# A ninth pair of the down product by seven products, with other low parts made by adding DMA

## The chip, the cores and the metric

The kernel runs on one core of a Trainium2 chip. The metric is the device time in microseconds (us). Before the change it is 286.42 us, the median of 3 runs (286.15 to 286.48). Beside it stands one profiled execution of 286.22 us, whose span from the first to the last instruction is 284.4 us; all rows of the trace come from that execution.

## The reference

One decoder layer in float32, for 256 tokens of width 1024: RMS norm, an input projection, eight heads of causal attention beside a convolution module, an output projection, and then the part that is changed, a SwiGLU feed-forward of width 2816:

```python
h = rms_norm(x, norm2_g[l])
x = x + (jax.nn.silu(h @ w_gate[l]) * (h @ w_up[l])) @ w_down[l]
```

## The kernel before, in words

**Split operands.** TensorE gets each float32 operand as two parts: a high part, which ScalarE makes by rounding (`activation(..., Copy)` into a float32r tile), and a low part, the original minus the high part. A product is then three matmuls: high by high, high by low, low by high. Each weight needs one rounding on ScalarE (L265 in `feed`, L200 in `split`) and one low part. The low part is made in one of two ways (`low_part`): VectorE subtracts (L219), or, for the pieces in the list `BY_DMA`, ScalarE writes the negated high part (L216) and a DMA issued by POOL adds the original to it (L217). The original comes from DRAM (`home`).

**Pieces and places.** The weights come from DRAM in blocks of 128 x 2048 through four buffers (`raw`). A piece is 128 x 1024. Pieces 0 to 71 belong to the projections and to gate and up; those from 72 (`DOWN`) on belong to the down product. Eight places (`WGT`) hold the split pieces; a new piece takes the place of the lowest numbered one, and ScalarE's rounding into it waits until TensorE has read that one for the last time. `feed(upto)` issues the roundings up to one piece past `upto` and the subtractions up to `upto`. `turns` is the order in which the pieces get their places: the number, except that a piece listed in `BEHIND` goes right behind the piece named there, to give its adding DMA time. Every engine executes in program order.

**Gate and up.** 22 blocks f of 128 feed-forward columns, 16 pairs of matmuls each. `glu_task` runs beside them: VectorE adds the halves of the gate (`tg`) and multiplies by the norm's factor, ScalarE makes silu of `tg` in a tile `sf`, VectorE adds the halves of the up product and multiplies by `sf`.

**The down product.** 11 pairs of feed-forward blocks. Seen as a product of 2 x 2 blocks (two halves of the tokens, two blocks of the pair, two halves of the 1024 columns), a pair marked P in `PAIRS` ("plain") is eight block products, 24 matmuls of 512 columns, and has two pieces. A pair marked F ("fast") is seven block products (`seventh`), 21 matmuls, with sums of blocks as operands. On the weights' side these sums are made by VectorE from the block of the pair in three instructions (`add_up`, L234 to L236, one of 1024 and two of 512 columns) into one of two buffers. A fast pair has three pieces, the raw second half of its block (a = 0) and the two halves of the sums (a = 1, 2), and the block's first quarter is split by itself (`single`, L200 and L201, into `b11` or `other`). On the activations' side, VectorE makes five sums (L869 to L871) and ScalarE and VectorE split seven operand forms (L875, L878); a plain pair has two splits instead (L860, L862). In the down product the pairs are run in order, 0 to 10. A fast pair takes its products in three groups; for all but the last fast pair the first group has the two products with piece a = 0 and then the first quarter's. The last fast pair, number 9, begins with the first quarter's product (M1), and then takes one with piece a = 1. Pair 10 is plain and is run last, one output block after the other, and VectorE adds each finished block to the residual stream (L981) while POOL adds others (L986). Ahead of these stand two sums of finished products on VectorE (L995, L997).

With `PAIRS = "FFFPFFFPFFP"` the pieces are 72 to 74 for pair 0, 75 to 77, 78 to 80, 81 and 82 for pair 3, 83 to 85, 86 to 88, 89 to 91, 92 and 93 for pair 7, 94 to 96, 97 to 99, 100 and 101 for pair 10. In the down product the issue order around pair 7 is: sums of pair 6, low parts 90, 91, 93, sums of pair 8, low part 94, quarter of pair 8, low parts 95 and 96, sums of pair 9, low part 97, quarter of pair 9, low parts 98 to 101.

Of the kernel before, what the change touches and what calls it, by code (L numbers as in the profile page):

```python
# [8 lines left out]
F32 = mybir.dt.float32  # L9
# [3 lines left out]
AF = mybir.ActivationFunctionType  # L13
ALU = mybir.AluOpType
AX = mybir.AxisListType

P = 128
D = 1024
T = 256
# [38 lines left out]
V_PIECE = 21  # L58
SS_WAIT = 2
OUT_LATE = 6  # L60
PAIRS = "FFFPFFFPFFP"
FAST = [p for p in range(NF // 2) if PAIRS[p] == "F"]
PLAIN = [p for p in range(NF // 2) if PAIRS[p] == "P"]
DOWN = 72
BEHIND = {75: 70, 78: 72, 81: 75, 82: 78, 83: 78, 86: 80, 89: 83, 92: 86}
BY_DMA = [*range(45, DOWN, 3), *BEHIND]
FAR = 46
SUMS = {66: 0, 69: 1}
FORMS_LATE = 11
# [72 lines left out]
def _build(nc, tc, t, ctx):  # L142
# [45 lines left out]
    def load_block(i, between=None):  # L188
        if i >= NB:
            return  # L190
        r = raw.tile([P, BW], F32, name=f"raw{i}", tag="raw")
        n = BW // (2 if between else 1)
        for j in range(BW // n):
            if j:
                between()
            nc.sync.dma_start(r[:, j * n:(j + 1) * n], t["w"][i - 2][:, j * n:(j + 1) * n])
        blocks[i] = r
# [5 lines left out]
    def new_piece():  # L203
        j = turns[len(pieces)]
        z = places.index(min(places))
        places[z] = j
        pieces[j] = [wgt.tile([P, PIECE], F32R, name=f"w{s}{j}", tag=f"w{s}{z}") for s in "hl"]
        i, a = divmod(j * PIECE, BW)
        if j >= DOWN:
            return pieces[j], down_piece(*down[j - DOWN]), j  # L210
        return pieces[j], blocks[i][:, a:a + PIECE] if i > 1 else None, j

    def low_part(dst, src, by_dma=False):

        if by_dma:
            nc.scalar.activation(dst[1], dst[0].bitcast(F32), AF.Copy, scale=-1.0)  # L216
            nc.gpsimd.dma_start(dst[1], src.bitcast(F32R), accum_op=ALU.add)  # L217
        else:
            nc.vector.tensor_tensor(dst[1], src, dst[0].bitcast(F32), op=ALU.subtract)  # L219
# [5 lines left out]
    index = {d: DOWN + a for a, d in enumerate(down)}  # L225
    turns = sorted(range(DOWN + len(down)), key=lambda j: BEHIND[j] + 0.5 if j in BEHIND else j)
    wsums, b11 = {}, {}
# [19 lines left out]
    def home(j):  # L247

        i, a = divmod(j * PIECE, BW)
        if j >= DOWN:  # L250
            p, a = down[j - DOWN]
            i, a = DOWN // 2 + p, (a if p in PLAIN else 1) * PIECE
        return t["w"][i - 2][:, a:a + PIECE]

    def single(q):

        i = DOWN // 2 + FAST[q]
        split(b11[q % 3], blocks[i][:, 0:W], nc.vector)
        load_block(i + RAW)

    def feed(upto, more=1):
        last = DOWN + len(down) - 1
        while len(pieces) <= min(upto + more, last):
            dst, src, j = new_piece()
            nc.scalar.activation(dst[0], src, AF.Copy)  # L265
            if j in BY_DMA:
                low_part(dst, home(j), True)
            waiting.append((dst, src, j))
            waiting.sort(key=lambda w: w[2])
        while waiting and waiting[0][2] <= upto:  # L270
            dst, src, j = waiting.pop(0)
            if j not in BY_DMA:
                low_part(dst, src)
            if j < DOWN and j % 2:
                load_block(j // 2 + RAW)
            elif j >= DOWN and down[j - DOWN][0] in FAST[2:] and down[j - DOWN][1] == 0:
                single(FAST.index(down[j - DOWN][0]))
            elif j >= DOWN and down[j - DOWN][0] in PLAIN and down[j - DOWN][1]:
                load_block(DOWN // 2 + down[j - DOWN][0] + RAW)
# [19 lines left out]
    def halves(out, bank, side):  # L299

        nc.scalar.activation(side, bank[:, T:], AF.Copy)
        nc.vector.tensor_tensor(out, bank[:, 0:T], side, op=ALU.add)
# [80 lines left out]
    for kt in range(KT):  # L383
        if kt % 2 == 0:
            dst, _, _ = new_piece()
# [260 lines left out]
    def ln_task():  # L646
# [5 lines left out]
        for i in (1, 0):  # L652
            b = t_bank(f"cv{i}", "s")
            for j in range(2):
                o = j * T + i * P
                mm3(b, [m[:, o:o + P] for m in inv], G["ys"][j], j == 0, i == 1 and j == 1)
            if i == 0:
                mm3(b, [m[:TAIL + 1, 2 * T:] for m in inv], G["ys"][2], False, True)
                cv[i] = b
            else:  # L660
                cv[i] = work("cvb", "tmp", 6)
                nc.vector.tensor_tensor(cv[i], b, G["glub"][:, 2, :], op=ALU.add)
            nc.vector.bn_stats(st[:, i, :], cv[i])
            nc.vector.bn_aggr(mv[:, i, :], st[:, i, :])
            if i:
                feed(V_PIECE + 1)
# [31 lines left out]
    for chunk in range(5):  # L698
        banks = [mm_bank(f"p{chunk}{i}") for i in range(NT)]
        for kt in range(KT):  # L700
            step()
            ahead = unit // 2 + 1 if unit < L1 else (unit + 3) // 2 if unit < L2 else unit // 2 + 3
            feed(ahead if unit < V_UNIT else min(ahead, V_PIECE))
            if unit == L1 - 1:
                feed(ahead + 1, 0)
            w = wtile(unit * W, W)
            unit += 1
            sls = [slice(i * P, (i + 1) * P) for i in range(NT)]
            order = [(i, a) for a in (0, 2, 1) for i in range(NT)]
            for i, a in order:  # L710
                nc.tensor.matmul(banks[i], (xh, xh, xl)[a][:, kt, sls[i]], w[a % 2], start=kt == 0 and a == 0,  # L711
                                 stop=kt == KT - 1 and a == 1)
        if after[chunk]:
            spawn(after[chunk](banks))
# [74 lines left out]
    for d in range(8):  # L789
# [3 lines left out]
        if d == 0:  # L793
            early_ctx.close()
            late = ffn["late"] = pool("late")
# [22 lines left out]
    late = ffn["late"]  # L818
# [19 lines left out]
    def glu_task(f, pg, pu):  # L838
        tg = late.tile([P, T], F32, name=f"tg{f}", tag="tg", bufs=2)
        halves(tg, pg, side(f"gs{f}"))  # L840
        nc.vector.tensor_tensor(tg, tg, r_bc, op=ALU.mult)
        s = late.tile([P, T], F32, name=f"sf{f}", tag="sf", bufs=2)
        yield 1
        nc.scalar.activation(s, tg, AF.Silu)
        yield max(1, ffn["up"][f] - now[0])
        pair, second = divmod(f, 2)
        if pair in PLAIN:
            ac = late.tile([P, T], F32, name=f"ac{f}", tag="ac")
        else:
            q = FAST.index(pair)  # L850
            if q not in pair_sums:
                pair_sums[q] = late.tile([P, 9 * P], F32, name=f"ps{q}", tag="ps")
            ps = pair_sums[q]
            ac = ps[:, 0:T] if second else ps[:, T:2 * T]
        halves(ac, pu, side(f"us{f}"))
        nc.vector.tensor_tensor(ac, ac, s, op=ALU.mult)
        if pair in PLAIN:
            a = 2 * PLAIN.index(pair) + second
            yield 1
            nc.scalar.activation(acts[:, 0, a, :], ac, AF.Copy)  # L860
            yield 1
            nc.vector.tensor_tensor(acts[:, 1, a, :], ac, acts[:, 0, a, :].bitcast(F32), op=ALU.subtract)  # L862
        elif second:
            if q == len(FAST) - 1:
                yield FORMS_LATE


            p3 = ps.rearrange("p (b q) -> p b q", q=P)
            nc.vector.tensor_tensor(p3[:, 4:6], p3[:, 2:4], p3[:, 0:2], op=ALU.subtract)  # L869
            nc.vector.tensor_tensor(p3[:, 6:8], p3[:, 5:6].to_broadcast([P, 2, P]), p3[:, 2:5:2], op=ALU.subtract)  # L870
            nc.vector.tensor_tensor(p3[:, 8], p3[:, 2], p3[:, 3], op=ALU.subtract)  # L871
            yield 1
            parts = ((forms[q][:, :, 0:3], p3[:, 0:3]), (forms[q][:, :, 3:7], p3[:, 5:9]))
            for to, of in parts:
                nc.scalar.activation(to[:, 0], of, AF.Copy)  # L875
            yield 1
            for to, of in parts:
                nc.vector.tensor_tensor(to[:, 1], of, to[:, 0].bitcast(F32), op=ALU.subtract)  # L878
# [4 lines left out]
    for f in range(NF):  # L883
# [5 lines left out]
        a = 0  # L889
# [20 lines left out]
        if f == 0:  # L910
            spawn(glu_task(0, pg, pu), GLU0_WAIT)
            ffn["up"][0] = now[0] + GLU0_WAIT
# [78 lines left out]
    m1, u1, u2, s = (rest[:, a, :] for a in range(4))  # L991
# [74 lines left out]
```

## Time and profile before

| | us | |
|---|---|---|
| median of the runs | 286.42 | 3 runs |
| profiled execution | 286.22 | one run |
| its span | 284.4 | |
| TensorE (PE) busy | 280.3 | 99% of the span |
| VectorE (DVE) busy | 236.0 | 83% |
| ScalarE (ACT) busy | 202.4 | 71% |
| POOL busy | 43.4 | 15% |
| DMA by the adding queue (POOL's) | | 18.0% of 16 engines' span |

A row in order of time has the start in us, the time taken, the engine, the line, the operation, what it writes and reads, and a count; in brackets stands the idle time ahead of it and what ended it. The low part of a weight is `wl`, the high part `wh`, the sums of a fast pair's weights `t`, the first quarter's parts `b11h`, `b11l` or, in the last pairs, `other`. The two parts of an operand of the activations are in `forms`, `other` or `act`.

### The profile page before, as it was taken

The page shows a single profiled execution, that of the slowest core. Times are in us where ns is not written, and L with a number is a line of the kernel's source. Part 1 is how long each engine was busy: PE and PEld are TensorE (multiplying, and loading weights), DVE is VectorE, ACT ScalarE, POOL GpSimd, SP SyncE. Part 2 cuts the span into 40 slices and gives each one's busy share as a digit, 9 for nine tenths or more (in the row PEclk, how much of TensorE's full clock was granted, in tenths as well). Part 3 has the DMA queues.
Part 4 walks back from the last instruction along what each step waited for, and adds up shares of the span by engine and source line. Part 5 has one row for each costly group of instructions (what it writes and reads, how often), then busy time and mean ns, then how long its engine had stood idle before and what let it go on. Part 6 is the DMA issues. An engine that isn't in the chain of part 4 may idle for free.

```text
span 284.4 us, 4150 instructions
## 1 busy us (share of the span) xinstructions
PE 280.3 (99%) x1466; PEld 235.0 (83%) x1466; DVE 236.0 (83%) x420; ACT 202.4 (71%) x331; POOL 43.4 (15%) x71
## 2 busy tenths in 40 slices
PE   8999999999999999999999999999999999999995
PEld 6887877778788888888888888888888888888884
DVE  4879996896894969999967687697489889999994
ACT  5857688986728677467878777776777799856640
POOL 0004555423000000000111111001111121200042
PEclk9999999999999999999999999999999999999999
DMA  7999958846204870746699998998996679994003
GB/s 265 381 421 367 410 178 291 316 156 213 84 0 149 309 277 7 296 151 235 214 305 293 304 288 229 279 285 218 332 214 158 179 241 281 267 303 186 0 0 148
DMA packets 12918, 65.62 MB, mean 231 GB/s; under 512 B 1697, under 2 KB 2305, under 8 KB 7266
## 3 DMA queue, kind: packets, MB, share of 16 engines
q1 hardware_dynamic: 10018, 55.14, 52.7%
q0 software_dynamic: 2736, 10.22, 18.0%
q8 instruction: 11, 0.18, 0.3%
q14 instruction: 9, 0.07, 0.1%
q10 hardware_dynamic: 144, 0.00, 0.0%
HBM read 64.31 MB, written 1.05 MB: 230 GB/s over the span
## 4 chain that ended last, share of the span: by engine, by line
PE 99%; DVE 0%; issue 0%
PE p L711 20%; PE sum L935 19%; PE fg L294 14%; PE fu L294 14%; PE po L757 8%; PE fg L296 7%; PE fu L296 7%; PE warm L356 1%; PE S L545 1%; PE pT L575 1%; PE O L731 1%; PE xT L770 1%; PE cv L305 0%; PE cv L307 0%; PE hf L305 0%; PE cv L306 0%
## 5 line engine op out<-in xcount | busy, mean ns | idle before, releaser
L265 ACT ACTIVATE wh<-raw 128x1024 fp32r<-128x1024 f32 x82 | 84.8, 1053 | 16.4 <-PE fu L294 7.8
L219 DVE TENSOR_TENSOR wl<-raw,wh 128x1024 fp32r<-128x1024 f32 x65 | 78.3, 1219 | 3.4 <-ACT wh L265 3.4
L294 PE MATMUL fu<-g,wh 128*128 128x512 f32 x176 | 62.5, 395 | 0.0
L294 PE MATMUL fg<-g,wh 128*128 128x512 f32 x176 | 62.4, 394 | 0.0
L296 PE MATMUL fg<-g,wl 128*128 128x256 f32 x176 | 48.8, 277 | 0.0
L296 PE MATMUL fu<-g,wl 128*128 128x256 f32 x176 | 48.8, 277 | 0.0
L217 POOL DMA_DIRECT2D wl<-w x17 | 14.7, 865 | 166.0 <-PE fu L296 70.8
L294 PEld LDWEIGHTS fg<-g,wh 128*128 128x128 f32 x176 | 33.0, 187 | 7.7
L294 PEld LDWEIGHTS fu<-g,wh 128*128 128x128 f32 x176 | 33.0, 188 | 7.6
L296 PEld LDWEIGHTS fg<-g,wl 128*128 128x128 f32 x176 | 33.1, 188 | 0.0
L296 PEld LDWEIGHTS fu<-g,wl 128*128 128x128 f32 x176 | 33.1, 188 | 0.0
L711 PE MATMUL p<-wh,xh 128*128 128x512 f32 x80 | 25.9, 405 | 0.0
L935 PE MATMUL sum<-wh,forms 128*128 128x512 f32 x84 | 25.8, 389 | 0.0
L711 PE MATMUL p<-wl,xh 128*128 128x512 f32 x80 | 24.9, 392 | 0.0
L711 PE MATMUL p<-wh,xl 128*128 128x512 f32 x80 | 24.8, 391 | 0.0
L265 ACT ACTIVATE wh<-t 128x1024 fp32r<-128x1024 f32 x16 | 16.9, 1057 | 9.4 <-PE sum L935 5.3
L219 DVE TENSOR_TENSOR wl<-t,wh 128x1024 fp32r<-128x1024 f32 x16 | 19.4, 1221 | 0.2
L216 ACT ACTIVATE wl<-wh 128x1024 fp32r<-128x1024 f32 x17 | 18.0, 1061 | 0.5
L935 PEld LDWEIGHTS sum<-wh,forms 128*128 128x128 f32 x84 | 15.7, 188 | 3.2
L711 PEld LDWEIGHTS p<-wh,xh 128*128 128x128 f32 x80 | 14.4, 190 | 4.2 <-issue 1.3
L711 PEld LDWEIGHTS p<-wl,xh 128*128 128x128 f32 x80 | 14.8, 188 | 3.6 <-DVE wl L219 0.5
L711 PEld LDWEIGHTS p<-wh,xl 128*128 128x128 f32 x80 | 15.0, 188 | 3.3
(203 smaller groups left out, 478.7 us busy)
## 6 DMA issues: line engine op xcount, KB each, us to landing
raw<-w SPq DMA_DIRECT2D x44, 1024.0 KB, 6.8
wl<-w POOLq DMA_DIRECT2D x17, 512.0 KB, 9.0
first<-first SPq DMA_DIRECT2D x8, 384.0 KB, 5.7
raw<-w SPq DMA_DIRECT2D x2, 512.0 KB, 7.1
xtok<-xtok SPq DMA_DIRECT2D x2, 512.0 KB, 9.7
x<-xtok SPq DMA_DIRECT2D x2, 512.0 KB, 6.6
c_rows<-rows SPq DMA_DIRECT2D x1, 768.0 KB, 11.0
out<-x SPq DMA_DIRECT2D x3, 256.0 KB, 2.0
```

Source lines behind the costliest of these rows:

```text
L216: nc.scalar.activation(dst[1], dst[0].bitcast(F32), AF.Copy, scale=-1.0)
L217: nc.gpsimd.dma_start(dst[1], src.bitcast(F32R), accum_op=ALU.add)
L219: nc.vector.tensor_tensor(dst[1], src, dst[0].bitcast(F32), op=ALU.subtract)
L265: nc.scalar.activation(dst[0], src, AF.Copy)
L294: nc.tensor.matmul(out.rearrange("p (a q) -> p a q", a=2), w[0], both, start=z in first and z not in seen, stop=False)
L296: nc.tensor.matmul(out[:, 0:T], w[1], both[:, 0, :], start=False, stop=z in last and left[z] == 0)
L356: nc.tensor.matmul(warm[:, 0:T], ones[:, 0:P], ones, start=True, stop=True)
L545: nc.tensor.matmul(banks[a][:, out], G["qT"][rows, j, q], G["kT"][rows, j, k], start=True, stop=True)
L575: nc.tensor.transpose(b[:, a * P:(a + 1) * P], p[:, a * P:(a + 1) * P], ident)
L711: nc.tensor.matmul(banks[i], (xh, xh, xl)[a][:, kt, sls[i]], w[a % 2], start=kt == 0 and a == 0, stop=kt == KT - 1 and a == 1)
L757: nc.tensor.matmul(po[i, n], G["mix"][l][:, k, i * P:(i + 1) * P], w[r], start=k == a == 0, stop=k == KT - 1 and a == 2)
L935: nc.tensor.matmul(banks[m], lhs, rhs, start=first, stop=last)
```

## The change

Pair 7 becomes a fast pair, so there are nine of them, 103 pieces instead of 102, and the pieces from 94 on have other meanings: 92 to 94 are pair 7, 95 to 97 pair 8, 98 to 100 pair 9, 101 and 102 pair 10. The low parts of 95 and 98 (the first pieces of pairs 8 and 9) are made by adding DMA, and these pieces go behind 89 and 92. Those of 73 and 74 (the sums of pair 0) are made by adding DMA too, with the sums in SBUF as the original, since they have no home in DRAM; `home` returns nothing for them and `feed` passes the tile. Those of 66 and 69 go back to VectorE. Silu writes over its argument `tg`, and the tile `sf` is gone.

With it the issue order on VectorE behind the low parts 90 and 91 is: quarter of pair 7, sums of pair 7, low parts 93 and 94, quarter of pair 8, sums of pair 8, low parts 96 and 97, sums of pair 9, quarter of pair 9, low parts 99 to 102. ScalarE rounds piece 99 ahead of the quarter of pair 9.

```diff
-PAIRS = "FFFPFFFPFFP"
+PAIRS = "FFFPFFFFFFP"
...
-BEHIND = {75: 70, 78: 72, 81: 75, 82: 78, 83: 78, 86: 80, 89: 83, 92: 86}
-BY_DMA = [*range(45, DOWN, 3), *BEHIND]
+BEHIND = {75: 70, 78: 72, 81: 75, 82: 78, 83: 78, 86: 80, 89: 83, 92: 86, 95: 89, 98: 92}
+BY_DMA = [*range(45, 64, 3), 73, 74, *BEHIND]
...
             p, a = down[j - DOWN]
+            if a and p in FAST:
+                return None
...
             if j in BY_DMA:
-                low_part(dst, home(j), True)
+                low_part(dst, home(j) or src, True)
...
-        s = late.tile([P, T], F32, name=f"sf{f}", tag="sf", bufs=2)
         yield 1
-        nc.scalar.activation(s, tg, AF.Silu)
+        nc.scalar.activation(tg, tg, AF.Silu)
...
-        nc.vector.tensor_tensor(ac, ac, s, op=ALU.mult)
+        nc.vector.tensor_tensor(ac, ac, tg, op=ALU.mult)
```

## Prediction, made before the changed kernel ran

> **What bounds the kernel now.** I read the page first, then the busy time by stage, then each engine in order of time from the moment the down product starts.
>
> ```profile
> PE 280.3 (99%) x1466; PEld 235.0 (83%) x1466; DVE 236.0 (83%) x420; ACT 202.4 (71%) x331; POOL 43.4 (15%) x71
> PE 99%; DVE 0%; issue 0%
> ```
>
> Over the whole span TensorE is the bound: it is busy 280.3 of 284.4 us, and the chain that ended last is TensorE for 99%. VectorE at 83% seems to have room. The table by stage (columns: stretch, its length, then busy us and count of PE, PEld, DVE, ACT, POOL) shows where it has none.
>
> ```profile
> 104.00:210.00 106.00, 106.00 (x615) 92.75 (x615) 84.19 (x160) 79.26 (x132) 8.67 (x10) 1.00 0.80 241
> 226.00:240.00 14.00, 14.00 (x64) 11.64 (x63) 13.01 (x22) 13.60 (x21) 2.59 (x3) 1.00 0.87 248
> 240.00:273.00 33.00, 33.00 (x147) 27.33 (x146) 32.50 (x35) 22.24 (x25) 1.72 (x2) 1.00 0.60 180
> ```
>
> In the gate and up products (first row) VectorE idles 21.8 of 106 us. In the down product from 240 to 273 it is busy 32.5 of 33: a second engine as full as TensorE, which makes the weights' low parts and the sums that the seven products need. As long as each low part is ready before its matmul, TensorE does not show it.
>
> ```profile
> 226.57 53.05 PE sum L935 x234
> ```
>
> From the chain: 234 matmuls of 512 columns in 53.05 us, 0.227 us each (a single one is shown with 0.39 in the rows below, because they overlap). Three matmuls are one product, 0.68 us.
>
> **The change, part by part.** *Pair 7 by seven products.* 24 matmuls become 21. TensorE gains 3 x 0.227 = 0.68 us, whole if nothing waits. The price is on VectorE: pair 7's block has to be added up, its first quarter split, and it has three pieces instead of two. The pieces after 92 are renumbered: pair 7 is 92 to 94, pair 8 95 to 97, pair 9 98 to 100, pair 10 101 and 102. VectorE's order in the second half of the down product, before:
>
> ```profile
> 251.55 1.22 DVE L234 TENSOR_TENSOR t<-raw 128x1024 f32<-128x1024 f32 x1
> ...
> 254.14 2.50 DVE L219 TENSOR_TENSOR wl<-t,wh 128x1024 fp32r<-128x1024 f32 x2
> 256.56 1.22 DVE L219 TENSOR_TENSOR wl<-raw,wh 128x1024 fp32r<-128x1024 f32 x1
> 257.69 1.22 DVE L234 TENSOR_TENSOR t<-raw 128x1024 f32<-128x1024 f32 x1
> ...
> 261.42 0.68 DVE L201 TENSOR_TENSOR b11l<-raw,b11h 128x512 fp32r<-128x512 f32 x1
> 262.02 2.36 DVE L219 TENSOR_TENSOR wl<-t,wh 128x1024 fp32r<-128x1024 f32 x2
> 264.29 1.22 DVE L234 TENSOR_TENSOR t<-raw 128x1024 f32<-128x1024 f32 x1
> ...
> 268.61 2.35 DVE L219 TENSOR_TENSOR wl<-t,wh 128x1024 fp32r<-128x1024 f32 x2
> 270.88 2.35 DVE L219 TENSOR_TENSOR wl<-raw,wh 128x1024 fp32r<-128x1024 f32 x2
> 273.61 0.69 DVE L995 TENSOR_TENSOR rest<-sum,rest 128x512 f32<-128x512 f32 x1 [0.37 <-PE sum L935]
> ...
> 274.94 3.00 DVE L981 SCALAR_TENSOR_TENSOR x<-sum,rstd,x 128x512 f32<-128x512 f32 x4
> 278.30 0.75 DVE L981 SCALAR_TENSOR_TENSOR x<-sum,rstd,x 128x512 f32<-128x512 f32 x1 [0.36 <-PE sum L935]
> 279.73 0.75 DVE L981 SCALAR_TENSOR_TENSOR x<-sum,rstd,x 128x512 f32<-128x512 f32 x1 [0.68 <-PE sum L935]
> 280.44 0.48 DVE L981 SCALAR_TENSOR_TENSOR x<-sumleft,rstd,x 128x256 f32<-128x256 f32 x1
> 281.09 0.48 DVE L981 SCALAR_TENSOR_TENSOR x<-sumright,rstd,x 128x256 f32<-128x256 f32 x1 [0.16 <-PE sumright L935]
> ```
>
> From start to start: an adding up (three instructions) 254.14 - 251.55 = 2.59; two low parts right behind it 2.42; a first quarter 262.02 - 261.42 = 0.60; a single low part 257.69 - 256.56 = 1.13. The adding up at 251.55 is pair 6's in both kernels, since the rows of the order differ only behind it. Before, what follows it up to the last low part is 90, 91, 93, adding up of pair 8, 94, quarter of 8, 95, 96, adding up of 9, 97, quarter of 9, 98 to 101.
>
> *95 and 98 by adding DMA.* They are the first pieces of pairs 8 and 9, on VectorE before (as 94 and 97). So the new order holds one low part fewer (-1.13), one adding up (+2.59) and one quarter (+0.60) more: about +2.1 us on an engine with 0.5 us of slack in 33. On ScalarE the two negated copies and the larger pair go into 10.8 idle us of that stage; POOL, busy 1.7 us there, takes the issues.
>
> Step by step: adding up of 6 at 251.55; 90 and 91 at 254.14; quarter of 7 at 256.56; adding up of 7 at 257.16; 93 and 94 at 259.75; quarter of 8 at 262.17; adding up of 8 at 262.77; 96 and 97 at 265.36; adding up of 9 at 267.78; then the quarter of 9 at 270.37 and 99 at 270.97.
>
> Who waits: pair 9 on TensorE, which takes the first-quarter product first and then one with the first sum.
>
> ```profile
> 270.62 0.84 PE L935 MATMUL sum<-other 128*128 128x512 f32 x3
> 271.30 0.61 PE L935 MATMUL sum<-wh,other 128*128 128x512 f32 x2
> 271.75 0.39 PE L935 MATMUL sum<-wl,other 128*128 128x512 f32 x1
> ```
>
> Before, low part 98 was done at 268.61 + 1.22 = 269.83 and needed at 271.75: 1.9 us to spare. Now pair 9 is due at 270.62 - 0.68 = 269.94. ScalarE, in its own order, rounds the piece made of the first sum and then the quarter:
>
> ```profile
> 265.62 1.06 ACT L265 ACTIVATE wh<-t 128x1024 fp32r<-128x1024 f32 x1 [3.12 <-PE sum L935]
> 266.59 0.61 ACT L200 ACTIVATE other<-raw 128x512 fp32r<-128x512 f32 x1
> ```
>
> The rounding at 265.62 follows the first addition (264.29 + 1.22); the 3.12 us are put down to TensorE, but it was that sum that came last. The quarter is rounded by 267.20, 2.91 after the adding up began. Now that is 267.78 + 2.91 = 270.69, and TensorE waits 0.75 us for it. The quarter's low part takes VectorE from 270.7 to 271.4, where the third matmul wants it at 271.14: 0.26 more. Low part 99 runs from 271.3 to 272.5, wanted at 271.4 + 3 x 0.227 = 272.08: 0.44 more. Low part 100 (272.4 to 273.65) is wanted at 273.9 and waits for nothing. TensorE loses 0.75 + 0.26 + 0.44 = 1.45 and ends 1.45 - 0.68 = 0.77 us later than before.
>
> VectorE then ends even later. 100, 101 and 102 start at 272.43, 273.56 and 274.69, and the first instruction of the end at 275.82 instead of 273.61. The rows of the end, with their waits gone, are 1.33 (273.61 to 274.94), 3.00, 0.75, 0.75, 0.48 and 0.48: done at 282.61 against 281.57. That is +1.04 us, and the output DMA follows it as before.
>
> *73 and 74 by DMA, 66 and 69 not.* This takes 2.3 us of low parts off VectorE at 218 to 221, just ahead of the down product. I count it as nothing, since the engines meet again behind it:
>
> ```profile
> 235.97 1.04 ACT L265 ACTIVATE wh<-raw 128x1024 fp32r<-128x1024 f32 x1
> 237.04 1.06 ACT L216 ACTIVATE wl<-wh 128x1024 fp32r<-128x1024 f32 x1
> 238.01 0.61 ACT L200 ACTIVATE b11h<-raw 128x512 fp32r<-128x512 f32 x1
> ```
> ```profile
> 235.71 0.39 PE L935 MATMUL sum<-wl,forms 128*128 128x512 f32 x1
> ```
> ```profile
> 238.66 0.69 DVE L201 TENSOR_TENSOR b11l<-raw,b11h 128x512 fp32r<-128x512 f32 x1
> 240.34 1.22 DVE L234 TENSOR_TENSOR t<-raw 128x1024 f32<-128x1024 f32 x1
> ```
>
> Piece 86 at 235.97 takes the place of 76, whose last reader is the last matmul of pair 1, at 235.71. So ScalarE cannot round it sooner, nor negate it, nor round the quarter at 238.01, and VectorE's quarter at 238.66 waits for that. From there the order is the old one up to 251.55, so a VectorE that comes earlier only idles. Bounds: a gain of up to 2.3 us if this meeting point gave way, and 1.0 of loss if piece 74 lands late (below). I take 0, which the rows at 235.71 and 235.97 put nearest. Low parts 66 and 69 return to VectorE between 190 and 204, with pair 7's new operand forms (at most five instructions, each under the 1.22 of a low part): up to 8.5 us into 21.8 idle ones. If that cover were gone they would add those 8.5 us to VectorE, not to TensorE, whose operands are made several pieces ahead.
>
> *Silu over its argument.* No instruction goes or comes. The argument's buffer is held until the up product is multiplied in; the next writer of that buffer stands behind this multiplication in VectorE's own order. 0 us either way, at most the lateness of one instruction shorter than a low part's 1.22, which the 21.8 idle us take.
>
> Sum: -0.68 + 1.45 on TensorE, and +0.27 more for VectorE's end: +1.04. The profiled execution was 286.22 us, so 287.26; that execution is 0.20 under the runs' median of 286.42, so 287.4 for the median. A change within 0.2% (0.57 us) of it can't be told from none.
>
> **Rivals.** *VectorE keeps up (faster).* If the 2.3 us saved at 218 carry through to pair 9, nothing waits and the 0.68 us come whole: 285.7. It decides at 1.45 us earlier on VectorE by 267.8. For it speaks VectorE's idle time of 1.0 us in 226 to 240; against it the meeting point at 235.97. The Trainium skill, Perfetto Trace Analysis, section Identifying the Most-Contended Engine, would have one optimise first the engine with the highest occupancy; by the whole page that is TensorE, and its cut would come whole, though its section Optimization Strategy says that the most contended engine can change between regimes. The rows by stage bear out the second.
>
> *Part of it (same).* The low parts behind an adding up take 2.27 instead of 2.42 (262.02 to 264.29), and VectorE gets a part of its earlier start through: 0.5 to 1.0 us less delay, 286.4 to 286.9.
>
> *Piece 74 lands late (slower still).* Its low part now comes from a DMA that adds the sum held in SBUF.
>
> ```profile
> 218.18 1.06 ACT L265 ACTIVATE wh<-t 128x1024 fp32r<-128x1024 f32 x1
> ```
> ```profile
> L217 POOL DMA_DIRECT2D wl<-w x17: 851/861/925, 138.1 to 247.1; - x17
> DMA to landing us min/median/max: 5.5/9.0/11.0
> ```
> ```profile
> 230.27 0.39 PE L935 MATMUL sum<-wl,forms 128*128 128x512 f32 x1
> ```
>
> Rounded by 219.24, negated by 220.3 and issued then, it lands at 225.8, 229.3 or 231.3; TensorE wants it at 230.27. The longest landing costs 1.0 us on top of the rest, since all later places and pieces follow TensorE: 288.4. Against it speaks the median, which leaves 1.0 us to spare; for it, that no transfer here reads SBUF and adds. The Trainium skill, SBUF - State Buffer, section Who interferes with whom, says that a VectorE instruction with two SBUF inputs contends with a POOL instruction that reads SBUF, but not with one that only writes it. The 17 issues between 851 and 925 ns, beside a VectorE full of such instructions, agree that issuing is not held up.
>
> **How the numbers follow.** Pair 9 waits and VectorE ends late: 0.63, 287.4, own range 287.0 to 288.0. Part of it: 0.17. VectorE keeps up: 0.10. Piece 74 late: 0.10, 288.0 to 289. The range 286.2 to 288.4 leaves out the faster case and the worst of the last. Faster 0.11, within 0.2% 0.19, slower 0.70.
>
> **What would show it.** Right: a gap of about 1.5 us on TensorE at the start of pair 9, before a matmul that reads the quarter in the late buffer; ScalarE's rounding of it near 270; VectorE without idle time from 240 to the end; the adding up of pair 6 at 251.55 as before; pair 7 on TensorE from 260.4 to 265.2. Wrong: an adding up of pair 6 well ahead of 251.55, which means that the meeting point moved; a gap on TensorE near 230, which means the DMA; or no gap at all.

## The result and the profile after

The changed kernel takes 288.43 us (median of 6 runs, 288.16 to 289.52) against 286.24 us for the kernel before beside it (6 runs, 285.98 to 286.48). The ratio is 1.0082, 95% interval 1.0065 to 1.0099: slower by 2.2 us, where 1.0 us was forecast (287.4, with 288.4 as the upper end). The profiled execution is 288.16 us with a span of 286.3 us, 1.94 us over the profiled one of before.

The first lines of the page and its chain that ended last:

```profile
PE 280.8 (98%) x1463; PEld 234.5 (82%) x1463; DVE 239.3 (84%) x426; ACT 206.3 (72%) x335; POOL 46.0 (16%) x73
PE 84%; DVE 7%; DMA 4%; issue 2%; ACT 1%; POOL 0%; ACTq 0%; POOLq 0%
```

Three matmuls are gone and TensorE's busy time has not fallen. The chain, 99% TensorE before, is 84% TensorE now and runs through VectorE, a DMA and ScalarE too. The same stages as before:

```profile
104.00:210.00 106.00, 106.00 (x616) 92.79 (x615) 87.53 (x165) 77.51 (x130) 6.95 (x8) 1.00 0.76 231
226.00:240.00 14.00, 13.62 (x61) 10.97 (x60) 12.00 (x21) 12.85 (x18) 2.60 (x3) 1.00 1.05 300
240.00:273.00 33.00, 32.16 (x141) 26.01 (x140) 31.06 (x35) 23.22 (x26) 3.45 (x4) 1.00 0.78 208
```

The gate and up products carry the low parts 66 and 69 and pair 7's forms without a wait: VectorE 3.3 us busier, TensorE full. In the down product TensorE has gaps in both stretches, and VectorE, which should have been without idle time from 240 on, is busy 1.4 us less than before: it waits too. TensorE's waits in the whole span (engine, line, what it waited for: us in total, times, longest), the start of the kernel left out:

```profile
PE sum L936 <- ACT other L200: 0.8, 1, 0.8
...
PE sum L936 <- DMA wl<-t: 0.4, 1, 0.4
PE sum L936 <- DVE wl L219: 0.2, 1, 0.2
```

Where they stand, in order of time:

```profile
230.89 0.50 PE L936 MATMUL sum<-wl,forms 128*128 128x512 f32 x1 [0.38 <-DMA wl<-t]
231.22 0.63 PE L936 MATMUL sum<-wh,forms 128*128 128x512 f32 x2
...
271.71 1.23 PE L936 MATMUL sum<-other 128*128 128x512 f32 x3 [0.84 <-ACT other L200]
272.77 0.62 PE L936 MATMUL sum<-wh,other 128*128 128x512 f32 x2
273.57 0.50 PE L936 MATMUL sum<-wl,other 128*128 128x512 f32 x1 [0.17 <-DVE wl L219]
```

The first is piece 74's low part in pair 0. The others are the start of pair 9, as forecast: the quarter's high part from ScalarE, then the low part of 99 from VectorE. But pair 9 starts at 271.71, not at the 270.69 of the prediction. VectorE's order shows why:

```profile
251.55 1.22 DVE L234 TENSOR_TENSOR t<-raw 128x1024 f32<-128x1024 f32 x1
...
255.28 2.36 DVE L219 TENSOR_TENSOR wl<-t,wh 128x1024 fp32r<-128x1024 f32 x2 [1.06 <-ACT wh L267]
...
266.35 2.50 DVE L219 TENSOR_TENSOR wl<-t,wh 128x1024 fp32r<-128x1024 f32 x2
268.77 1.22 DVE L234 TENSOR_TENSOR t<-raw 128x1024 f32<-128x1024 f32 x1
...
271.69 0.69 DVE L201 TENSOR_TENSOR other<-raw,other 128x512 fp32r<-128x512 f32 x1 [0.25 <-ACT other L200]
272.30 2.35 DVE L219 TENSOR_TENSOR wl<-t,wh 128x1024 fp32r<-128x1024 f32 x2
...
276.84 0.68 DVE L996 TENSOR_TENSOR rest<-sum,rest 128x512 f32<-128x512 f32 x1
...
283.04 0.48 DVE L982 SCALAR_TENSOR_TENSOR x<-sumright,rstd,x 128x256 f32<-128x256 f32 x1 [0.17 <-PE sumright L936]
```

The adding up of pair 6 starts at 251.55, to the hundredth as before. But the low parts 90 and 91 start at 255.28 instead of 254.14: 1.06 us of waiting for ScalarE, which stay in the order to the end (adding up of pair 9 at 268.77, forecast 267.78; first instruction of the end at 276.84, forecast 275.82). On ScalarE, at that time:

```profile
252.15 1.06 ACT L267 ACTIVATE wh<-raw 128x1024 fp32r<-128x1024 f32 x1 [1.85 <-DMA raw<-w]
253.24 1.06 ACT L216 ACTIVATE wl<-wh 128x1024 fp32r<-128x1024 f32 x1
254.21 1.99 ACT L267 ACTIVATE wh<-t 128x1024 fp32r<-128x1024 f32 x2
```

The rounding at 252.15 is piece 95, which the change moves ahead of 90. It is cut from pair 8's block, and that block was still on its way from DRAM. Behind it in ScalarE's order stand its negated copy and then the roundings of 90 and 91 (254.21, both), for which VectorE waits.

### The profile page after: what moved, and what is told of

It reads as the page before. It is cut to its first block, busy times and chain, and to the rows that moved or that the text cites. A ratio compares the mean times of both kernels' runs of the same rounds, so it can differ in the third digit from the quotient of the medians.

```text
span 286.3 us, 4164 instructions
## 1 busy us (share of the span) xinstructions
PE 280.8 (98%) x1463; PEld 234.5 (82%) x1463; DVE 239.3 (84%) x426; ACT 206.3 (72%) x335; POOL 46.0 (16%) x73
## 4 chain that ended last, share of the span: by engine, by line
PE 84%; DVE 7%; DMA 4%; issue 2%; ACT 1%; POOL 0%; ACTq 0%; POOLq 0%
PE p L713 20%; PE fg L296 12%; PE sum L936 12%; PE fu L296 12%; PE po L759 8%; PE fg L298 6%; PE fu L298 6%; DMA wl<-t 4%; DVE wl L219 2%; DVE t L234 2%; PE warm L358 1%; PE S L547 1%; ACT wh L267 1%; PE pT L577 1%; DVE t L235 1%
## 5 line engine op out<-in xcount | busy, mean ns | idle before, releaser
L219 DVE TENSOR_TENSOR wl<-raw,wh 128x1024 fp32r<-128x1024 f32 x64 | 77.1, 1218 | 3.4 <-ACT wh L267 3.3
L936 PE MATMUL sum<-wh,forms 128*128 128x512 f32 x96 | 29.6, 389 | 0.0
L267 ACT ACTIVATE wh<-t 128x1024 fp32r<-128x1024 f32 x18 | 18.9, 1054 | 7.4 <-DVE t L234 5.5
L936 PEld LDWEIGHTS sum<-wh,forms 128*128 128x128 f32 x96 | 18.0, 188 | 3.7
L216 ACT ACTIVATE wl<-wh 128x1024 fp32r<-128x1024 f32 x19 | 20.2, 1061 | 0.6
L936 PE MATMUL sum<-wl,forms 128*128 128x512 f32 x48 | 18.8, 392 | 0.4 <-DMA wl<-t 0.4
```

The lines of the kernel that those rows point to most:

```text
L936: nc.tensor.matmul(banks[m], lhs, rhs, start=first, stop=last)
```

## The experiments

Every run was timed beside the kernel before, whose median was 286.04 to 286.31 us. The diffs are against the changed kernel, unless the text says otherwise.

**Data that is there.** Pieces 95 and 98 read a block that landed earlier, and nothing else moves.

```diff
-        w = blocks[DOWN // 2 + p]
+        w = blocks[DOWN // 2 + p - (a == 0 and p in (8, 9))]
...
-            i, a = DOWN // 2 + p, (a if p in PLAIN else 1) * PIECE
+            i, a = DOWN // 2 + p - (a == 0 and p in (8, 9)), (a if p in PLAIN else 1) * PIECE
```

> The changed kernel, in which pieces 95 and 98 read the block of the pair before theirs (7 and 8), which has landed long since; the amount of work on every engine is the same, only the output differs. Theory (the missing part of the loss is ScalarE's wait of 1.85 us for the raw block of pair 8 at 252.15, which holds back the roundings of 90 and 91 and VectorE by 1.06 us): that wait is gone, pair 6's low parts start at 254.1 instead of 255.3, pair 9's first matmul comes about 1.0 us earlier (270.7), and the time falls by 0.9 to 1.0 us, to 287.4 to 287.6 (ratio to the kernel before about 1.004). Rival (the late piece 74 near 230 is the missing part): no change, 288.4.

Measured: 287.16 us, ratio 1.0036 (1.0024 to 1.0048). ScalarE rounds 95 at once, and VectorE's low parts 90 and 91 follow their sums without a wait (below, with VectorE's order to its end):

```profile
250.27 1.04 ACT L267 ACTIVATE wh<-raw 128x1024 fp32r<-128x1024 f32 x1
```
```profile
254.22 2.49 DVE L219 TENSOR_TENSOR wl<-t,wh 128x1024 fp32r<-128x1024 f32 x2
...
267.84 1.22 DVE L234 TENSOR_TENSOR t<-raw 128x1024 f32<-128x1024 f32 x1
...
275.91 0.69 DVE L996 TENSOR_TENSOR rest<-sum,rest 128x512 f32<-128x512 f32 x1
...
282.10 0.48 DVE L982 SCALAR_TENSOR_TENSOR x<-sumright,rstd,x 128x256 f32<-128x256 f32 x1 [0.15 <-PE sumright L936]
```

The theory holds. By the ratios the wait is worth 0.0046 of 286 us, 1.3 us, a little more than expected; in the trace VectorE ends 0.94 us sooner (282.58 against 283.52), which is what was expected. What is left over the kernel before, 0.36% or 1.03 us (0.88 between the medians), is about the sum of the prediction (1.04), which had left out this wait.

**The sums of pair 0 on VectorE.**

```diff
-BY_DMA = [*range(45, 64, 3), 73, 74, *BEHIND]
+BY_DMA = [*range(45, 64, 3), *BEHIND]
```

> The changed kernel with the low parts of 73 and 74 on VectorE. Theory (VectorE's and ScalarE's order sets pair 9, so a gap on TensorE at 230 only takes the place of waiting at pair 9): the gap at 230.9 goes, TensorE is 0.55 us earlier up to pair 9 and waits there as much longer, the time stays at 288.3 to 288.5. Rival (the gap at 230 counts in full): 287.8 to 287.9. Second rival (low parts on VectorE at 218 to 221 hold back the whole chain): 289 or more.

Measured: 289.12 us, ratio 1.0099 (1.0085 to 1.0113). The gap at 230 is gone, and TensorE waits at pair 9 instead:

```profile
272.40 1.23 PE L936 MATMUL sum<-other 128*128 128x512 f32 x3 [1.51 <-ACT other L200]
```
```profile
252.84 1.06 ACT L267 ACTIVATE wh<-raw 128x1024 fp32r<-128x1024 f32 x1 [2.23 <-DMA raw<-w]
```

So the gap at 230 does not set the changed kernel's time: with it or without it, pair 9 starts when ScalarE has the quarter. But the time did not stay, as the theory had it. It is 0.6 us above its expectation, in the range of the second rival (289 or more). That rival's reason, the low parts at 218 to 221, is not what this trace shows: its rows are 0.24 us later than those of the changed kernel already near 204 (204.62 against 204.38) and 0.33 later at the start of the down product, so at most 0.09 arises between. Pair 9 starts 0.69 later (272.40 against 271.71): these 0.33, and 0.4 because the load of pair 8's block took 9.4 us instead of 9.0. The same load took 9.3 in the kernel before and in the run with pair 9 in the other order, so it differs by about that much from trace to trace. Why the rows are late from early on, no run told.

**Pair 7 plain again.**

```diff
-PAIRS = "FFFPFFFFFFP"
+PAIRS = "FFFPFFFPFFP"
...
-BEHIND = {75: 70, 78: 72, 81: 75, 82: 78, 83: 78, 86: 80, 89: 83, 92: 86, 95: 89, 98: 92}
+BEHIND = {75: 70, 78: 72, 81: 75, 82: 78, 83: 78, 86: 80, 89: 83, 92: 86}
```

> The changed kernel with pair 7 plain again (eight products, 95 and 98 as before the change), so that what is left of the change is 73 and 74 by adding DMA, 66 and 69 on VectorE, and silu over its argument. Theory: TensorE waits 0.4 to 0.6 us for piece 74 near 230.9 and nowhere else, since pair 9 had 1.9 us to spare; all later work follows TensorE: 286.7 to 286.9 (ratio 1.002). If the later waits came from these edits and not from pair 7: 288.

Measured: 286.94 us, ratio 1.0016 (1.0004 to 1.0027): 0.46 us by the ratio, 0.66 between the medians. One wait on TensorE in the down product, the same as in the changed kernel, and here it counts, since nothing later waits:

```profile
230.72 0.50 PE L936 MATMUL sum<-wl,forms 128*128 128x512 f32 x1 [0.38 <-DMA wl<-t]
```

**The sums of pair 9 on POOL.**

```diff
+            eng = nc.gpsimd if q == len(FAST) - 1 else nc.vector
...
-            nc.vector.tensor_tensor(u[:, 0:2 * W], w[:, 0:2 * W], w[:, W:3 * W], op=ALU.add)
+            eng.tensor_tensor(u[:, 0:2 * W], w[:, 0:2 * W], w[:, W:3 * W], op=ALU.add)
```

(and so the two other additions)

> The changed kernel, in which POOL, not VectorE, adds up the block of pair 9 (three instructions, 2.6 us of VectorE). Theory (VectorE's work ahead of pair 9 is the price of the ninth pair): VectorE comes to the quarter of pair 9 at 268.8 instead of 271.7, TensorE finds it ready, and only the wait near 230.9 stays: -0.68 + 0.55, so 286.0 to 286.3. Rival (two engines that add from the same memory slow one another, so that nothing is won): 287.5 to 289.

Measured: 291.75 us, ratio 1.0196 (1.0180 to 1.0211). The rival holds, and by more than it said. VectorE's adding up of pair 8 and POOL's of pair 9 ran beside one another; VectorE first:

```profile
264.01 3.42 DVE L235 TENSOR_TENSOR t<-raw 128x1024 f32<-128x1024 f32 x1
267.46 1.66 DVE L236 TENSOR_TENSOR t<-t,raw 128x512 f32<-128x512 f32 x1
269.15 1.64 DVE L237 TENSOR_TENSOR t<-t,raw 128x512 f32<-128x512 f32 x1
```
```profile
263.58 2.77 POOL L235 TENSOR_TENSOR t<-raw 128x1024 f32<-128x1024 f32 x1 [2.65 <-DVE wl L219]
```

Additions of 1.22 and 0.69 us take 3.42, 1.66 and 1.64. So this run says nothing on whether less work on VectorE would help; it had more: 6.7 us for the sums of pair 8 alone, where two pairs take 5.2 in the changed kernel. The Trainium skill, SBUF - State Buffer, section Who interferes with whom, says that a VectorE instruction with two SBUF inputs contends with a POOL instruction that reads SBUF. The trace agrees (3.42 us against 1.22).

**Pair 9 in the order of the other pairs.**

```diff
-            groups = ((M2, N3, M1), (N5, M7), (M6, N4)) if q < len(FAST) - 1 else ((M1, N5), (M7, M6), (M2, N3, N4))
+            groups = ((M2, N3, M1), (N5, M7), (M6, N4))
```

> The changed kernel with pair 9's products in the order of the other fast pairs: first the two with piece 98, which is ready, and only then the first quarter's. TensorE's due times for the quarter and for low part 99 move back by 1.36 us. Theory (VectorE's own order up to the last residual add ends as late as TensorE): TensorE's wait at pair 9 shrinks from about 1.2 to 0.3 us, but VectorE's end stays where it is, and the time with it: 288.1 to 288.5. Rival (TensorE's wait at pair 9 is the whole price): 287.3 to 287.6.

Measured: 288.25 us, ratio 1.0073 (1.0059 to 1.0086), not to be told from the changed kernel. The last rows of TensorE and of VectorE:

```profile
282.03 0.28 PE L936 MATMUL sumright<-wl,act 128*128 128x256 f32 x1
```
```profile
283.45 0.48 DVE L982 SCALAR_TENSOR_TENSOR x<-sumright,rstd,x 128x256 f32<-128x256 f32 x1
```

TensorE is done at 282.31 and VectorE at 283.93, with no idle time ahead of its last rows (changed kernel: 283.00 and 283.52). In this trace VectorE's first instruction of the end is 0.67 us later than in the changed kernel (277.51 against 276.84): 0.36 stand there from the start of the down product on, and pair 8's block took 9.3 us instead of 9.0. It ends only 0.41 later, so the new order saves about 0.26 us behind that instruction, an estimate from these two traces. TensorE's wait at pair 9 is a sign, and little of the price: the price is VectorE's order, which reaches to the last residual add.

**Silu alone** (against the kernel before).

```diff
-        nc.scalar.activation(s, tg, AF.Silu)
+        nc.scalar.activation(tg, tg, AF.Silu)
```

> The kernel before with silu over its argument and nothing else. Every theory: no change, 286.1 to 286.5 (ratio 0.999 to 1.001). If it is slower by 0.5 us or more, the buffer's later release holds the gate's adds back.

Measured: 286.39 us, ratio 0.9998 (0.9987 to 1.0009). Nothing, as expected.

**The ninth pair, with the old lists of pieces made by DMA** (against the kernel before; silu over its argument is in it too).

```diff
-PAIRS = "FFFPFFFPFFP"
+PAIRS = "FFFPFFFFFFP"
```

> The kernel before with pair 7 by seven products and silu over its argument (for the memory), the pieces made by DMA as before the change: 66 and 69 yes, 73, 74, 95 and 98 no. VectorE has two low parts more ahead of pair 9 than in the changed kernel, but no rounding waits for raw data and no late DMA stands at 230. Theory: pair 9 waits about 3 us, the end moves by 3.0 us: 289.0 to 289.6. Rival (the moved DMA pieces are the cost, and the ninth pair is not): 286.5 or less.

Measured: 290.37 us, ratio 1.0139 (1.0126 to 1.0153), 4.0 us. The direction and the rows are the theory's, the size is 0.8 us above it; 0.3 of this stands in the trace ahead of the down product (a row of ScalarE at 204.60, before at 204.31). Pair 9 waits for both parts of its quarter:

```profile
272.21 0.73 PE L936 MATMUL sum<-other 128*128 128x512 f32 x2 [1.08 <-ACT other L200]
273.70 0.50 PE L936 MATMUL sum<-other 128*128 128x512 f32 x1 [0.76 <-DVE other L201]
```

The ninth pair alone costs 4.0 us, and the low parts that the change moves win back 1.6 us of it by the ratios (1.9 between the medians), net of the waits for raw data and for piece 74. That this is mostly the work of 95 and 98, which stand ahead of pair 9 in VectorE's order, is argued; no run moves them alone.

**Three suspects out at once**: the earlier block for 95 and 98, the sums of pair 0 on VectorE, and pair 7's block not added up.

```diff
+        if p == 7:
+            return w[:, (2 * a - 2) * W:2 * a * W]
         add_up(FAST.index(p))
```

> The changed kernel without its three suspected costs at once: pieces 95 and 98 read the block of the pair before theirs (no wait for raw data), pair 7's block isn't added up (its pieces 93 and 94 are read from the raw block; 2.6 us less on VectorE), and the low parts of 73 and 74 are on VectorE (no late DMA). The output differs. Theory: nothing waits on TensorE after 226, three matmuls fewer come whole: -0.68 us, 285.5 to 285.8 (ratio 0.9976). Rival (pair 9 would wait anyway, for a fourth reason such as ScalarE): 286.2 or more.

Measured: 286.18 us, ratio 1.0002 (0.9993 to 1.0011). The theory fails here and the rival is right, down to the engine:

```profile
255.58 1.05 ACT L269 ACTIVATE wh<-raw 128x1024 fp32r<-128x1024 f32 x1
256.66 1.06 ACT L216 ACTIVATE wl<-wh 128x1024 fp32r<-128x1024 f32 x1
257.62 2.00 ACT L269 ACTIVATE wh<-raw 128x1024 fp32r<-128x1024 f32 x2
```
```profile
258.70 2.36 DVE L219 TENSOR_TENSOR wl<-raw,wh 128x1024 fp32r<-128x1024 f32 x2 [1.68 <-ACT wh L269]
```

Piece 98, too, is placed early: its rounding and its negated copy (2.0 us) stand ahead of the roundings of 93 and 94, also where its data has landed. VectorE, relieved of 2.6 us, waits 1.68 us for them. In the changed kernel that is hidden under the adding up of pair 7. Here the wait reaches TensorE at pair 9:

```profile
269.73 1.02 PE L938 MATMUL sum<-other 128*128 128x512 f32 x3
...
271.39 0.50 PE L938 MATMUL sum<-wl,other 128*128 128x512 f32 x1 [0.17 <-DVE wl L219]
```

Six matmuls from 269.73 to 271.72, where the next one starts, are 1.99 us instead of 6 x 0.227 = 1.36. That is 0.63 us, nearly all of the 0.68 that the ninth pair wins.

**The ninth pair without sums for two pairs**: the kernel of the run with the old lists, and the blocks of pairs 7 and 8 not added up.

```diff
+        if p in (7, 8):
+            return w[:, (2 * a - 2) * W:2 * a * W]
         add_up(FAST.index(p))
```

> The ninth pair with the pieces made by DMA as before the change (e8_pair7_only), and the blocks of pairs 7 and 8 not added up: their pieces are read from the raw block, so the output differs, and VectorE has 5.2 us less to do ahead of pair 9. No piece is placed early beside those of before, so ScalarE holds nothing back. Theory (the three matmuls come whole as soon as VectorE has the time): no wait on TensorE after 226, 285.5 to 285.8, ratio 0.9970 to 0.9985. Rival (something besides VectorE's, ScalarE's and the DMA's lateness eats the 0.68 us, since leaving three costs out brought the time only to that of the kernel before): 286.2 or more.

Measured: 285.65 us beside 286.04, ratio 0.9987 (0.9976 to 0.9997). TensorE waits nowhere in the down product; its chain:

```profile
226.67 52.37 PE sum L938 x231
```

231 matmuls in 52.37 us are 0.227 each, as before, and three fewer. From the first matmul of pair 0 to the last of all are 53.97 us (226.50 to 280.47) against 54.64 before (226.41 to 281.05): 0.67 us, the forecast 0.68. The ratio's interval reaches from 0.09 to 0.69 us, so the whole of it is shown by the trace and not by the times. No run with the reference's whole work beat the kernel before.

## Why the prediction was right or wrong

**Right: what bounds the change.** VectorE, full in the down product, cannot take a fourth seven-product pair in a row; pair 9 waits for the quarter on ScalarE and then for low part 99; VectorE's end is as late as TensorE's. With the data in place the measured loss is 1.03 us (1.0036) against a sum of 1.04, and VectorE's rows are those of the forecast: the first instruction of the end at 275.91 (forecast 275.82), the last one done at 282.58 (282.61). (286.42 and 1.04 make 287.46; the prediction writes 287.4.) That TensorE's loss comes out too is luck. The sum has pair 9 pay all of its 1.45 us; in that run TensorE loses nearly 0.6 at piece 74 and comes to pair 9 that much later, so it loses only 0.95 there, 0.1 of it for the quarter's high part (forecast 0.75):

```profile
270.78 1.23 PE L936 MATMUL sum<-other 128*128 128x512 f32 x3
271.85 0.63 PE L936 MATMUL sum<-wh,other 128*128 128x512 f32 x2
272.65 0.50 PE L936 MATMUL sum<-wl,other 128*128 128x512 f32 x1 [0.17 <-DVE wl L219]
```

The rival *Part of it* rests on a row misread: the low parts at 262.02, 2.27 us, stand behind a quarter. Behind an adding up they take 2.42 in the changed kernel too (266.35 to 268.77).

**Wrong: the step "95 and 98 by adding DMA".** It set the two negated copies and the larger pair against 10.8 idle us on ScalarE, costed at nothing. It did not ask what stands behind the early rounding in ScalarE's order, nor whether its block would have landed. The wait of 1.85 us for pair 8's block held back 90 and 91 and put VectorE 1.06 us later; by times the step was worth 1.3 us. The idle time was there before, and the rounding was put into it; the data came at its end. Both could be read from the trace of before. ScalarE was idle from 250.3 to 252.86, and the load of pair 8's block, which takes the buffer of pair 4's and so follows its adding up (240.34 to 243.01), was issued at 243.07 and took 9.3 us: it landed at 252.4. The row of ScalarE, the row of the issue, and the load's size and us to landing:

```profile
252.86 1.06 ACT L265 ACTIVATE wh<-t 128x1024 fp32r<-128x1024 f32 x1 [2.57 <-DVE t L234]
```
```profile
243.07 0.33 SPq L196 DMA_DIRECT2D raw<-w  x1
```
```profile
raw<-w SPq DMA_DIRECT2D x1, 1024.0 KB, 9.3
```

In the changed kernel it was issued at 243.07 again and took 9.0.

**Half right: "Piece 74 lands late".** The event came. The row of its issue, and its transfer's size and us to landing:

```profile
220.70 0.87 POOL L217 DMA_DIRECT2D wl<-t  x1 [1.80 <-ACT gs L303]
```
```profile
wl<-t POOLq DMA_DIRECT2D x1, 512.0 KB, 10.1
```

It lands at 230.8 and TensorE takes it at 230.89 instead of about 230.3. The rival suspected the source in SBUF. The record leaves another reason open, that three adding DMAs now stand close together (issued at 218.03, 220.70 and 223.47): the third, whose source is in DRAM, took 9.5 us, where the same one took 5.5 before. But the rival's price was to come on top of the rest, and it doesn't: alone it costs 0.46 us by the ratio, and in the changed kernel pair 9 would have waited that time anyway.

**Right number, wrong reason: the meeting point.** That VectorE's head start of two low parts at 218 would be lost was right: 251.55 in both kernels. But piece 86 was not held by pair 1's last matmul. Piece 76, whose place it takes, is pair 1's second piece, and the last matmuls of a fast pair read its third. In the changed kernel pair 1 runs 0.7 us later, its last matmul starts at 236.48, and ScalarE rounds piece 86 at 235.97 all the same:

```profile
236.48 0.39 PE L936 MATMUL sum<-wl,forms 128*128 128x512 f32 x1
```

What holds ScalarE is its first row of the down product; the second row below is piece 86, at its old time:

```profile
226.68 0.63 ACT L200 ACTIVATE other<-raw 128x512 fp32r<-128x512 f32 x1 [1.25 <-PE fu L298]
...
235.97 1.05 ACT L267 ACTIVATE wh<-raw 128x1024 fp32r<-128x1024 f32 x1
```

The quarter goes into memory that held the activations (`other` has the tag `g2`, the name of the activations' tile), so it must wait for the last matmul of the up product. Before, ScalarE came there just in time; now it comes earlier and idles 1.25 us. The row of before:

```profile
226.69 0.62 ACT L200 ACTIVATE other<-raw 128x512 fp32r<-128x512 f32 x1
```

From there ScalarE's rows keep the same times in both, to 0.01 us, up to 238.53.

**Right: silu, 66 and 69, and the three matmuls.** Silu alone is 0.9998. The gate and up products show no wait. The 0.68 us are there when VectorE has the time.

## What to carry to other kernels

When a piece of work is moved earlier in an in-order engine's queue, ask two things of it: is its input there by then, and what stands behind it. Idle time on the engine doesn't answer either. Where a second engine is full beside the bounding one, cost a change by that engine's whole order, to its last instruction; the bounding engine's wait shows where it is felt, and removing that wait alone won some 0.3 us here, which the times can't tell from nothing.

## What the runs showed of the hardware

VectorE and POOL, adding in SBUF at once, lost more than the split of the work won: VectorE's additions of 1.22 and 0.69 us took 3.42 and 1.65 beside POOL's, and POOL's of 512 columns 2.15 and 1.60, against 1.30 (median) at the end of the changed kernel. After a wait, TensorE's next matmul takes longer: from 230.89 to the next start at 231.22 are 0.33 us instead of 0.227 in the changed kernel. The two adding DMAs whose source is in SBUF took 9.0 and 10.1 us, inside the 5.5 to 11.0 of those from DRAM. The load of pair 8's block, 1 MB issued between 242.8 and 243.6, took 8.8 to 9.7 us in the eleven traces.
